# First down projection with tokens as rows and seven block products for 8 of 22 pairs, weight sums in place, result turned back

## The chip, the cores and the metric

The kernel runs on one core of a Trainium2 chip. The metric is the device time of one execution in microseconds (us). TensorE (PE) does the matmuls, VectorE (DVE) and ScalarE (ACT) the elementwise work, GpSimd (POOL) and SyncE (SP) issue most of the transfers. PE reads its operands from SBUF and writes its sums to PSUM.

## The reference

The reference is a decoder trunk of two layers on 256 tokens of width D = 2048: gated linear attention, then block attention over a shared K/V, each followed by a gated feed-forward block with F = 5632 hidden channels. What the change touches is the down projection of the feed-forward block, and what stands behind the first of them:

```
def conv_ffn(x, norm_w, w_up, conv_w, conv_b, w_down):
    ...
    return (jax.nn.silu(a) * u) @ w_down          # (256, 5632) @ (5632, 2048)
...
h = h + conv_ffn(h, ...)                          # layer 0
k_blk, v_blk, k_mean = shared_kv(h, ...)
h = h + moba_mixer(h, ...)                        # layer 1: q = rms_norm(h) @ w_q first
h = h + conv_ffn(h, ...)                          # layer 1
```

All matrices are fp32. The kernel writes each fp32 factor as a high and a low fp32r part and takes three products (high times high, high times low, low times high) for each product of the reference.

## The kernel before, in words

**Weights.** `WeightStream` brings all weights through SBUF in one fixed order. A chunk is a 128x2048 raw tile (`wraw`, 3 buffers, one 1 MB transfer on SP's queue, L75). Each chunk gives two "halves" of 128x1024. A half is split into `whi` (a copy on ACT, L114) and `wlo` (a subtraction on DVE, L115); both come from a pool of 3 buffers. One call of `step()` hands one half to PE, and `prefetch` splits up to 2 halves ahead of PE (3 ahead in the last stage, where every fourth half has a buffer in the big pool instead). `step()` also runs jobs that `after(n, job)` has put down for n steps later.

**First down projection.** `project(rows(hid), FT, ...)` holds channels as rows. For each of 8 pairs of output blocks, `gemm` (L266 to L278) runs over 44 tiles of 128 hidden channels. Per tile and block there is one matmul of 512 columns (L275: 256 tokens high beside 256 tokens low, against `whi`) and one of 256 columns (L276: tokens high against `wlo`). That makes 704 of each. The weights are the stationary operand. After each pair, `residual` adds both PSUM parts to `h` (L309, L310), and `Norm.feed` makes the operand of the next stage, `xw` (ACT L208, DVE L209), and the sum of squares (ACT L218, DVE L219). `h` (8 tiles, in 4 slots) stays in SBUF for the whole kernel.

**The stage behind it.** The q projection is 4 calls of `gemm_tok`, 8 steps each. Step p of each call uses `xw` of pair p only: 12 matmuls of 512 columns (L290 to L292). Two steps in, `n.close` (L538) sums the squares for the norm; one step in, `bias_rows` (L596 to L615) starts. It loads `oh`, has PE make `biasrow` (L603), copies it on ACT (L605), sets part of it on DVE (L606), writes it to DRAM from POOL's queue (L608) and then gathers four tiles of 512 KB from there, also on POOL's queue (L612).

**Second down projection.** `last` (L748 to L811) already holds tokens as rows: the hidden tokens are the stationary operand and 512 columns of weights stream past. Output columns are cut in two blocks b of 1024, and the hidden tiles in 22 pairs k. A plain pair takes 8 block products of 3 matmuls each. In the 8 pairs of `SEVEN_PAIRS` the 2x2 blocks of tokens and weights take 7 products instead (a Strassen-Winograd scheme), so 21 matmuls in place of 24 (L769). This needs sums of token blocks (`combine`, made in the up projection for 4 pairs and at the start of the down projection for the other 4) and sums of weight blocks (`_sum`, L91, L93 and L94, into tiles of their own). A seven pair has four halves: `b11` (512 wide, 3 matmuls), and three of 1024 (6 matmuls each). PSUM holds six sums in the three `acc` tiles and two in the two `bank` tiles.

The order of instructions on each engine is made by a scheduler from the order in which the program is written, dependences and free buffers. Each engine runs its list in order.

Of the kernel before, what the change touches and what calls it, by code (L numbers as in the profile page):

```python
# [35 lines left out]
SEVEN_PAIRS = (1, 3, 6, 8, 11, 13, 16, 18)  # L36
SEVENS = [k in SEVEN_PAIRS for k in range(FT // 2)]
EARLY = 4


class WeightStream:
# [4 lines left out]
    def __init__(self, nc, raw, parts):  # L46
        self.nc, self.raw, self.parts = nc, raw, parts
        self.chunks, self.halves = [], []
        self.tiles, self.split = {}, {}
        self.n_dma = self.n_split = self.n_sum = 0  # L50
        self.cuts, self.lead = {}, {}
        self.sums, self.slot = {}, None
# [8 lines left out]
    def add_quads(self, w, g, kinds):  # L61

        for i, seven in enumerate(kinds):
# [17 lines left out]
    def _sum(self, upto):  # L81

        V = self.nc.vector
        while self.n_sum < min(upto, len(self.halves)):
            c, o, kind = self.halves[self.n_sum]
            if kind in ("t13", "t24"):
                self._dma(c + 1)
                src = self.tiles[c]
                t = self.slot([128, 1024], F32, kind)
                if kind == "t13":  # L90
                    V.tensor_sub(t, src[:, 512:1536], src[:, 0:1024])  # L91
                else:
                    V.tensor_add(t[:, :512], self.sums[self.n_sum - 1][:, 512:], src[:, :512])  # L93
                    V.tensor_sub(t[:, 512:], src[:, 1536:], t[:, :512])  # L94
                self.sums[self.n_sum] = t
            self.n_sum += 1

    def prefetch(self, i):
        nc = self.nc
        while self.n_split < len(self.halves):  # L100
# [5 lines left out]
            self._sum(n + 2)  # L106
            src = self.sums[n] if kind in ("t13", "t24") else self.tiles[c][:, o:o + 1024]
# [5 lines left out]
            for a, b in ((0, 512), (512, 1024)) if n == 0 else ((0, 512 if kind == "b11" else 1024),):  # L113
                nc.scalar.copy(hi[:, a:b], src[:, a:b])  # L114
                nc.vector.tensor_sub(lo[:, a:b], src[:, a:b], hi[:, a:b].bitcast(F32))  # L115
            self.split[n] = (hi, lo)
            self.sums.pop(n - 1, None)
# [11 lines left out]
def trunk(ctx: ExitStack, tc: tile.TileContext, xT, cst, msk, w1p, w2a, w_k, w_qa, w_v, w_g, w_go,  # L129
# [20 lines left out]
    def bank(name, shape):  # L150
# [4 lines left out]
            (w_up0, FT, 4096), (w_dn0, 8, FT * 256),  # L155
            (w_mq, 4, 8192), (w_kk, 4, 8192), (w_kv, 4, 8192), (w_mo, 8, 4096),
            (w_up1, FT, 4096)]
    for w, groups, cols in plan:
        for g in range(groups):
            ws.add(w, g, cols)  # L160
    for g in range(2):
        ws.add_quads(w_dn1, g, SEVENS)
# [396 lines left out]
    def ffn(layer, nrm, then):  # L559
# [5 lines left out]
        for j in range(FT):  # L565
# [18 lines left out]
            if layer == 1 and j % 2 and j // 2 in SEVEN_PAIRS[:EARLY]:  # L584
                combine(j // 2, whole)
        then(hid)

    n_ffn = Norm(C_FN, "xw")
# [143 lines left out]
    hscr = dram.tile([2, 128, D], F32, name="hscr")  # L732

    def turn_h(c, t):

        tp = bank("hT", (128, 512))
        for i in range(4):
            T.transpose(tp[:, 128 * i:128 * i + 128], h[2 * c + i // 2][:, i % 2, 128 * t:128 * t + 128], ident)
        x = temp("hT", (128, 512))
        A.copy(x, tp)  # L740
        nc.gpsimd.dma_start(hscr[t, :, 512 * c:512 * c + 512], x)

# [3 lines left out]

    def last(hid):
        for i, k in enumerate(SEVEN_PAIRS[EARLY:]):  # L748
            after(2 + 3 * i, lambda k=k: combine_parts(k, hid))
        for b in range(2):  # L750
            r = []
            for c in range(2):
                for t in range(2):
                    x = temp("res", (128, 512))
                    nc.gpsimd.dma_start(x, hscr[t, :, 1024 * b + 512 * c:1024 * b + 512 * c + 512])
                    r.append(x)
            two = [acc_ps.tile([128, 2, 512], F32, name="acc") for _ in range(3)]
            p = {n: two[i // 2][:, i % 2, :] for i, n in enumerate((1, 6, 5, 7, 2, 3))}
            p[4], p[8] = bank("p4", (128, 512)), bank("p8", (128, 512))
            left = {1: 0, 2: 0, 3: 0, 4: 0, 5: 0, 6: 0, 7: 0, 8: 0}  # L760
            for seven in SEVENS:
                for n in ((1, 5, 7, 6, 4, 3, 2) if seven else (2, 3, 4, 8, 2, 3, 4, 8)):
                    left[n] += 3
            begun = set()

            def prod(n, x, hi, lo):
                for xp, wp in ((x[0], hi), (x[0], lo), (x[1], hi)):
                    left[n] -= 1
                    T.matmul(p[n], xp, wp, start=n not in begun, stop=left[n] == 0)  # L769
                    begun.add(n)  # L770

            def part(k, i, t):
                x = hid[k][:, i, 128 * t:]
                return x[:, :128], x[:, S:S + 128]

            for k, seven in enumerate(SEVENS):
                if seven:
# [128 lines left out]
```

## Time and profile before

| what | us |
|---|---|
| time, median of 3 runs | 2247.14 (2246.71 to 2247.66) |
| the profiled execution, its own time | 2248.82 |
| span of its profile | 2246.7 |
| PE busy | 2226.4 (99%) |
| DVE busy | 1580.2 (70%) |
| ACT busy | 1232.8 (55%) |

The span is the time from the first to the last profiled instruction, the execution's own time is 2.1 us more. The profile page gives busy times by engine, the chain of work that ended last, and groups of instructions by source line. `us, mean ns | idle before` in a group are total busy time, the mean duration of one, and how long its engine stood still just before.

### The profile page before, as it was taken

The numbers are of one execution on the slowest core, as the hardware profiler recorded it, in microseconds if no ns is written. First come the engines' busy times: TensorE is split into PE (matmuls) and PEld (weight loads), VectorE is DVE, ScalarE is ACT, GpSimd is POOL, SyncE is SP. The second block draws the span as 40 slices with busy tenths as digits, with TensorE's granted clock in tenths as the row PEclk, the third lists the DMA queues.
The fourth block names the chain that finished last, engine by engine and source line by source line (L and its number), as shares of the span: only waits on it lengthen the run. The fifth ranks groups of instructions, "written<-read, shape, count | busy, mean of one in ns | idle before, by whom it ended". The sixth has DMA issues, their size and how long they took to land.

```text
span 2246.7 us, 30752 instructions
## 1 busy us (share of the span) xinstructions
PE 2226.4 (99%) x12146; PEld 1920.2 (85%) x12146; DVE 1580.2 (70%) x2151; ACT 1232.8 (55%) x1717; POOL 35.9 (2%) x43
## 2 busy tenths in 40 slices
PE   7999999999999999999999999999999999999999
PEld 6889888888888888888888888888888888887887
DVE  6566776777777777555557666567777777788876
ACT  6555654655555555444456565456556555555543
POOL 0000000000000000000011000000000000000000
PEclk9999999999999999999999999999999999999999
DMA  6554455555555555555565444456555555555654
GB/s 238 187 188 150 158 184 186 187 193 193 192 189 188 187 189 191 191 194 192 173 237 185 176 169 162 165 193 203 197 188 189 192 193 192 189 188 204 227 190 166
DMA packets 62739, 424.33 MB, mean 189 GB/s; under 512 B 7249, under 2 KB 7777, under 8 KB 13186
## 3 DMA queue, kind: packets, MB, share of 16 engines
q1 hardware_dynamic: 60210, 415.43, 52.3%
q0 software_dynamic: 1952, 6.37, 0.8%
q8 instruction: 95, 1.56, 0.3%
q10 hardware_dynamic: 432, 0.57, 0.1%
q14 instruction: 50, 0.41, 0.1%
HBM read 418.12 MB, written 4.22 MB: 188 GB/s over the span
## 4 chain that ended last, share of the span: by engine, by line
PE 97%; DVE 2%; DMA 1%; issue 0%; ACT 0%; DVEq 0%
PE acc L275 47%; PE acc L276 24%; PE acc L769 5%; PE acc L291 5%; PE acc L292 5%; PE acc L290 5%; PE p L769 3%; DVE wlo L115 1%; DMA wraw<-w_v 0%; PE sT L473 0%; PE tr L636 0%; DMA wraw<-w_dn 0%; PE s L654 0%; ACT whi L114 0%; PE pT L674 0%
## 5 line engine op out<-in xcount | busy, mean ns | idle before, releaser
L115 DVE TENSOR_TENSOR wlo<-wraw,whi 128x1024 fp32r<-128x1024 f32 (+1 forms) x785 | 948.2, 1212 | 550.8 <-ACT whi L114 544.1
L114 ACT CAST whi<-wraw 128x1024 fp32r<-128x1024 f32 (+1 forms) x785 | 814.9, 1042 | 865.6 <-PE acc L275 586.1
L275 PE MATMUL acc<-xw,whi 128*128 128x512 f32 x3328 | 1158.8, 393 | 0.0
L276 PE MATMUL acc<-xw,wlo 128*128 128x256 f32 x3328 | 928.5, 279 | 0.0
L275 PEld LDWEIGHTS acc<-xw,whi 128*128 128x128 f32 x3328 | 623.5, 187 | 141.7
L276 PEld LDWEIGHTS acc<-xw,wlo 128*128 128x128 f32 x3328 | 627.2, 188 | 0.2
L275 PE MATMUL acc<-hid,whi 128*128 128x512 f32 x704 | 244.1, 394 | 0.0
L276 PE MATMUL acc<-hid,wlo 128*128 128x256 f32 x704 | 195.0, 277 | 0.0
L275 PEld LDWEIGHTS acc<-hid,whi 128*128 128x128 f32 x704 | 132.0, 188 | 30.6
L276 PEld LDWEIGHTS acc<-hid,wlo 128*128 128x128 f32 x704 | 132.2, 188 | 0.0
L290 PE MATMUL acc<-whi,xw 128*128 128x512 f32 x256 | 100.7, 393 | 12.1 <-ACT xw L208 12.1
L291 PE MATMUL acc<-wlo,xw 128*128 128x512 f32 x256 | 101.0, 395 | 0.3 <-DVE wlo L115 0.3
L292 PE MATMUL acc<-whi,xw 128*128 128x512 f32 x256 | 100.7, 393 | 0.0
L291 PE MATMUL acc<-wlo,xkv 128*128 128x512 f32 x256 | 100.6, 393 | 0.0
L290 PE MATMUL acc<-whi,xkv 128*128 128x512 f32 x256 | 100.5, 393 | 0.0
L292 PE MATMUL acc<-whi,xkv 128*128 128x512 f32 x256 | 100.4, 392 | 0.0
L769 PE MATMUL acc<-whi,hid 128*128 128x512 f32 x288 | 100.3, 390 | 0.0
L572 ACT ACTIVATE au<-up,cs 128x256 f32<-128x256 f32 x176 | 95.9, 592 | 6.0 <-DVE up L568 6.0
L769 PE MATMUL p<-whi,hid 128*128 128x512 f32 x256 | 91.0, 392 | 0.1
L275 PE MATMUL acc<-go,whi 128*128 128x512 f32 x256 | 90.5, 399 | 0.0
L275 PE MATMUL acc<-ox,whi 128*128 128x512 f32 x256 | 89.1, 394 | 0.0
L574 DVE SCALAR_TENSOR_TENSOR au<-up,cs,au 128x255 f32<-128x255 f32 x176 | 76.9, 478 | 0.0
(238 smaller groups left out, 2231.3 us busy)
## 6 DMA issues: line engine op xcount, KB each, us to landing
wraw<-w_up SPq DMA_DIRECT2D x176, 1024.0 KB, 4.7
wraw<-w_dn SPq DMA_DIRECT2D x84, 1024.0 KB, 4.8
wraw<-w_g SPq DMA_DIRECT2D x16, 1024.0 KB, 4.8
wraw<-w_go SPq DMA_DIRECT2D x16, 1024.0 KB, 4.7
wraw<-w_mq SPq DMA_DIRECT2D x16, 1024.0 KB, 4.8
wraw<-w_kk SPq DMA_DIRECT2D x16, 1024.0 KB, 4.8
wraw<-w_kv SPq DMA_DIRECT2D x16, 1024.0 KB, 4.8
wraw<-w_mo SPq DMA_DIRECT2D x16, 1024.0 KB, 4.8
```

The source lines that it names most:

```text
L114: nc.scalar.copy(hi[:, a:b], src[:, a:b])
L115: nc.vector.tensor_sub(lo[:, a:b], src[:, a:b], hi[:, a:b].bitcast(F32))
L275: T.matmul(ps[:, b, :], hi[:, c:c + 128], x, start=kt == 0, stop=False)
L276: T.matmul(ps[:, b, :S], lo[:, c:c + 128], x[:, :S], start=False, stop=kt == kts - 1)
L290: T.matmul(ps[:, t, :], xh, wh, start=kt == 0, stop=False)
L291: T.matmul(ps[:, t, :], xh, wl, start=False, stop=False)
L292: T.matmul(ps[:, t, :], xl, wh, start=False, stop=kt == KT - 1)
L572: A.activation(au[:, i, :], t[:, i, :], AF.Identity, bias=col(cb + n), scale=col(cw + 2 * 2 * FT + n))
L574: V.scalar_tensor_tensor(au[:, i, 1:], t[:, i, :S - 1], col(cw + 2 * FT + n), au[:, i, 1:], op0=OP.mult, op1=OP.add)
L769: T.matmul(p[n], xp, wp, start=n not in begun, stop=left[n] == 0)
```

## The change

- The first down projection is written like the second one: tokens as rows, two blocks of 1024 output columns, 22 pairs, 8 of them with seven products in each block. Both use the new function `down`. The order of the pairs is written out in `ORDERS`; `+` marks a pair with seven products. In the second down projection the second block has 10 seven pairs, the first 8 as before.
- The weight sums are made in place in the raw tile (`_sums`, four operations of 512 columns on DVE). The halves of a seven pair are taken in another order: `b11`, `wide` (plain b22 and b21), `t13` (b12 and b22 after their sums), `t24` (b11 and b21 after theirs).
- `h` is written to DRAM during the first up projection (`park`, 8 transfers of 256 KB on POOL's queue) and its SBUF slots become free.
- The result of the first down projection has tokens as rows, while the next stage wants channels as rows. `back(q)` turns pair q with four PE transposes, loads the parked `h[q]` on POOL's queue, adds, and feeds the norm. For q = 0 to 3 (block 0) this runs inside block 1, for q = 4 to 7 one and two steps into the q projection. `nrm.close` runs 5 steps in.
- `EARLY`, the pairs whose token sums are made in the up projection, is (1, 3, 5, 7), now in both layers.
- In the second down projection the load of the residual stands behind the last seven pair of a block, no longer at the block's start.

```diff
+EARLY = (1, 3, 5, 7)
+ORDERS = [[_order("0 1+ 2 3+ 4 16 5+ 6 7+ 17 8 9+ 10 11+ 18 12 13+ 14 15+ 19 20 21"),
+           _order("0 2 4 6 8 10 1+ 12 3+ 14 5+ 16 7+ 17 9+ 18 11+ 19 13+ 20 15+ 21")],
+          [_order("0 1+ 2 3+ 4 16 5+ 6 7+ 17 8 9+ 10 11+ 18 12 13+ 14 15+ 19 20 21"),
+           _order("0 1+ 2 3+ 4 5+ 6 7+ 8 9+ 10 11+ 12 13+ 14 15+ 16 17+ 18 19+ 20 21")]]
...
-            self.halves += ([(c, 0, "b11"), (c, 0, "t13"), (c, 0, "t24"), (c, 1024, "wide")] if seven else
+            self.halves += ([(c, 0, "b11"), (c, 1024, "wide"), (c, 512, "t13"), (c, 0, "t24")] if seven else
...
+    def _sums(self, src):
+        V = self.nc.vector
+        b11, b12, b22, b21 = (src[:, 512 * i:512 * i + 512] for i in range(4))
+        V.tensor_sub(b22, b22, b12)
+        V.tensor_sub(b12, b12, b11)
+        V.tensor_add(b11, b22, b11)
+        V.tensor_sub(b21, b21, b11)
...
+    def down(layer, hid, ready, jobs):
+        done = set(EARLY)
+        for b, order in enumerate(ORDERS[layer]):
+            new = [k for k, seven in order if seven and k not in done]
+            done |= set(new)
+            todo = dict(jobs.get(b, {}))
+            for i, k in enumerate(new):
+                todo.setdefault(2 + 2 * i, []).append(late(k))
+            low = acc_ps.tile([128, 2, 512], F32, name="acc")
+            p = {2: low[:, 0], 3: low[:, 1], 4: bank("p4", (128, 512)), 8: bank("p8", (128, 512))}
...
+            for i, (k, seven) in enumerate(order):
+                for job in todo.get(i, ()):
+                    job()
+                if seven:
+                    prod(1, part(k, 0, 0), step(), 0)
+                    w = step()
+                    prod(3, comb(k, 3), w, 0)
+                    prod(2, part(k, 1, 0), w, 1)
...
+                else:
+                    for a in range(2):
+                        w = step()
+                        for n, t, f in ((2, 0, a), (3, 0, 1 - a), (4, 1, a), (8, 1, 1 - a)):
+                            prod(n, part(k, a, t), w, f)
+                if i == last:
+                    sums = ready(b, p)
+            ws.prefetch(cur[0])
+            sums(b, p)
...
+    def park(p):
+        nc.gpsimd.dma_start(hspill[p], h[p].rearrange("a b c -> a (b c)"))
+
+    def first_down(hid, nrm):
+        blocks = {}
+        def ready(b, p):
+            blocks[b] = r = u_sums(p, None)
+            def end(b, p):
+                for x, n in zip(r, (2, 3, 4, 8)):
+                    V.tensor_add(x, x, p[n])
+            return end
+
+        def back(q, where):
+            r = blocks[q // 4]
+            tp = where()
+            c, i0 = q % 4 // 2, q % 2 * 2
+            for i in range(2):
+                for t in range(2):
+                    T.transpose(tp[:, i, 128 * t:128 * t + 128],
+                                r[2 * t + c][:, 128 * (i0 + i):128 * (i0 + i) + 128], ident)
+            if q % 2 == 0:
+                hs[q // 2] = slot([128, 2, 2, S], F32, "h")
+            h[q] = hs[q // 2][:, q % 2]
+            nc.gpsimd.dma_start(h[q], hspill[q].rearrange("a (b c) -> a b c", b=2))
+            V.tensor_add(h[q], h[q], tp)
+            nrm.feed(q)
...
+        down(0, hid, ready, {1: {3 + q: [lambda q=q: back(q, in_acc)] for q in range(4)}})
+        for q in range(4, NP):
+            after(1 + (q - 4) // 2, lambda q=q: back(q, lambda: bank("hf", (128, 2, S))))
+        after(5, nrm.close)
...
     project(rows(go), KT, [n_ffn])
+    for p in range(NP):
+        after(6 + 2 * p, lambda p=p: park(p))
     n_q = Norm(C_MN, "xw", True)
-    ffn(0, n_ffn, lambda hid: project(rows(hid), FT, [n_q]))
+    ffn(0, n_ffn, lambda hid: first_down(hid, n_q))
```

More of the change, by code (lines that the diff above doesn't have):

```diff
@@ L105, in prefetch @@
             self._dma(c + 1)
-            self._sum(n + 2)
-            src = self.sums[n] if kind in ("t13", "t24") else self.tiles[c][:, o:o + 1024]
+            src = self.tiles[c]
+            if kind == "t13":
+                self._sums(src)
+            if kind == "t24":
+                src = src.rearrange("p (a b) -> p a b", a=4)[:, 0::3]
+            elif kind == "b11":
+                src = src[:, :512]
+            else:
+                src = src[:, o:o + 1024]
             if kind != "plain" and n % 4 == 3:
@@ L812, in trunk @@
-    ffn(1, n_ffn, last)
+    ffn(1, n_ffn, last_down)
 def _chunks(w):
```

213 lines of the change are left out of this document (108 added, 105 removed).

## The prediction

> **What bounds the kernel now.** I read the page first: engines, then the chain of work that ended last.
>
> ```profile
> span 2246.7 us, 30752 instructions
> PE 2226.4 (99%) x12146; PEld 1920.2 (85%) x12146; DVE 1580.2 (70%) x2151; ACT 1232.8 (55%) x1717; POOL 35.9 (2%) x43
> PE 97%; DVE 2%; DMA 1%; issue 0%; ACT 0%; DVEq 0%
> ```
>
> PE is busy for 99% of the span and holds 97% of the chain. So a matmul that goes is worth its full time, and a new wait of PE costs its full time. The profiled execution took 2248.82 us, 2.1 more than its span; the sums below stand against it. The median of the three runs, 2247.14, is 1.7 lower, and I give the result on that basis.
>
> Next the table of windows, for the four stages that the change touches: the first down projection, the head of the q projection, and start and middle of the second down projection (the number behind x counts instructions).
>
> ```profile
> core 0: us, PE busy (x) PEld busy (x) DVE busy (x) ACT busy (x) POOL busy (x), PEclk, DMA share, GB/s
> 885.88:1130.00 244.12, 244.12 (x1411) 213.50 (x1410) 129.00 (x131) 103.97 (x114) 0.51 (x1) 1.00 0.54 190
> 1130.00:1150.00 20.00, 20.00 (x91) 15.83 (x90) 11.06 (x15) 12.13 (x16) 3.52 (x5) 1.00 0.55 187
> 2005.60:2032.00 26.40, 23.63 (x94) 17.72 (x93) 26.09 (x44) 14.89 (x20) 0.54 (x1) 0.94 0.38 130
> 2032.00:2168.00 136.00, 136.00 (x601) 112.33 (x600) 111.88 (x121) 69.69 (x74) 2.15 (x4) 1.00 0.59 218
> ```
>
> The first down projection and the head of the q projection have no PE gap. DVE stands at 53% in the first, 82% in the middle of the second, and 99% in the start of the second, where PE falls short. So what the change brings into layer 0 is a stage with little DVE to spare. The waits of PE say that the start is the only place where the existing token-major form stalls:
>
> ```profile
> PE acc L769 <- DVE wlo L115: 2.0, 3, 1.1
> PE acc L769 <- ACT whi L114: 1.2, 1, 1.2
> ```
>
> **The change part by part: matmuls.** By tile `hid`:
>
> ```profile
> L275 PE MATMUL acc<-hid,whi x704: 392/394/395, 885.9 to 1129.6; 128*128 128x512 f32 x176
> L276 PE MATMUL acc<-hid,wlo x704: 274/277/280, 886.2 to 1129.9; 128*128 128x256 f32 x176
> ```
>
> The durations overlap, so I go by pace. Now: 704 pairs in 244.12 us. In the middle window of the second down projection 601 matmuls of 512 columns take 136.00 us, 0.2263 each. Without sevens the new form would have 2 x 22 x 24 = 1056 of them, 239.0 us, 5.1 less. Sixteen seven pairs save 3 each, 48 x 0.2263 = 10.9. Together **-16.0**. In the second down projection two more sevens save 6 x 0.2263 = **-1.4**.
>
> Turning back costs 32 transposes; the nearest row is eight in 0.87 us on the chain of waits, in order of time:
>
> ```profile
> 1138.34 0.74 PE biasrow L603 x2
> 1164.78 0.87 PE tr L636 x8
> ```
>
> 32 x 0.109 = **+3.5**. All removed, added and moved matmuls: **-13.9**.
>
> **Start of the down projection.** In 2005.60 to 2032.00 PE did 94 matmuls, worth 94 x 0.2263 = 21.3 us, in 26.4: 5.1 lost. Three gaps stand in the timeline of PE, and behind them a stretch with a lower granted clock:
>
> ```profile
> 2021.17 0.50 PE L769 MATMUL acc<-wlo,hid 128*128 128x512 f32 x1 [0.48 <-DVE wlo L115]
> ...
> 2024.72 0.51 PE L769 MATMUL acc<-whi,comb 128*128 128x512 f32 x1 [1.21 <-ACT whi L114]
> ...
> 2026.31 0.50 PE L769 MATMUL acc<-wlo,comb 128*128 128x512 f32 x1 [1.08 <-DVE wlo L115]
> ```
> ```profile
> 2027.60:2030.60 3.00, 3.00 (x8) 1.89 (x7) 3.00 (x4) 3.00 (x5) 0.00 (x0) 0.53 0.00 0
> ```
>
> The gaps add to 2.8 us, the clock of 0.53 takes the rest. DVE is the cause: the token sums of four late pairs are made there, each with rows like these:
>
> ```profile
> L556 DVE TENSOR_TENSOR whole<-hid x4: 683/691/693, 2013.9 to 2027.4; 128x512 f32<-128x512 f32 x4
> L544 DVE TENSOR_TENSOR comb<-whole x4: 281/288/293, 2017.1 to 2032.1; 128x128 f32<-128x128 f32 x4
> ```
>
> One late pair is 0.69 + four of 0.28 to 0.29 + a last subtraction of 512 columns, 0.69 (L314): 2.5 us, four pairs 10. The changed program asks for them at pairs 2, 4, 6, 8, but in its built order, in both layers alike, the scheduler puts all four right at the start again. Adding DVE's durations along that list and PE's at 0.2263, the `wlo` of the third pair is ready 2.4 us after PE wants it; the same addition on the kernel before gives 2.0 where 5.1 was measured. So layer 0, which has no such loss now, gets what layer 1 has: I take **+5.5** (bounds: 3, the gaps without the clock, to 8) and **+0.4** for layer 1.
>
> The Trainium skill, "TensorE: Matmul & The Clock Gate", Part 1: The HAM clock gate, says that the clock halves after an idle window of about 3.4 us. By it, gaps that are this short would cost no clock and the start would lose only its gaps, some 2 us less. The rows above speak against it: 0.53 was granted after gaps of at most 1.21 us.
>
> **Alternating pairs.** Behind the start a seven pair and a plain one follow each other. The rows for DVE and ACT:
>
> ```profile
> L115 DVE TENSOR_TENSOR wlo<-wraw,whi 128x1024 fp32r<-128x1024 f32 x767 | 936.3, 1224 | 548.3 <-ACT whi L114 541.6 <-PE acc L276 3.3 <-PE p L769 0.8
> L114 ACT CAST whi<-wraw 128x1024 fp32r<-128x1024 f32 x767 | 803.9, 1052 | 845.5 <-PE acc L275 585.6 <-PE acc L292 111.9 <-ACT au L572 56.6
> L115 DVE TENSOR_TENSOR wlo<-wraw,whi 128x512 fp32r<-128x512 f32 x18 | 12.3, 685 | 2.5 <-ACT whi L114 2.5
> L93 DVE TENSOR_TENSOR t<-t,wraw 128x512 f32<-128x512 f32 x16 | 10.9, 684 | 0.0
> ```
>
> A seven pair takes DVE 0.685 + 3 x 1.224 + 4 x 0.684 = 7.1 us, a plain one 2.45: 9.5. PE takes 45 x 0.2263 = 10.2. Four sums of 512 columns replace one of 1024 and two of 512 (0.2 more by these rows). In place, the first two sums must wait until `wide` has been read, and the copies of `t13` and `t24` wait for them: the chain sum, sum, copy (1.05), subtraction (1.22) is 3.6 us long, the six matmuls per 512-column half and the plain steps in front give 5 or more. It fits, with 1.3 to 1.4 us to spare per two pairs. In layer 1's second block two late pairs (17, 19) come in at 2.5 us each. I take **+1.5** for both layers; bounds 0, and 34 seven pairs x 0.2 = 7. The sums at block ends run on DVE and ACT under the next plain pairs (24 matmuls, 5.4 us, stand ahead of the reused p4, p8).
>
> Transfers of POOL's queue, by the table of DMA issues (the last number is the median time to landing):
>
> ```profile
> bias<-bscr POOLq DMA_DIRECT2D x4, 512.0 KB, 8.3
> hscr<-hT POOLq DMA_DIRECT2D x8, 256.0 KB, 5.2
> res<-hscr POOLq DMA_DIRECT2D x8, 256.0 KB, 3.8
> ```
>
> `park`'s eight transfers, like `hscr` in size and kind, are issued under up projection matmuls that don't read them, and layer 1's later residual load (`res`) has plain steps in front of its first reader: nothing for either, or, uncovered, the 3.8 us of one load.
>
> **The q projection** is where I see the largest new cost. Time 0 is its first matmul in the built order. A step is 12 x 0.2263 = 2.72. Steps 0 to 4 with 8 transposes end at 14.5, `biasrow` (0.74 above) at 15.2, step 5 with the transposes for pairs 6 and 7 at 18.8. Steps 6 and 7 need pairs 6, 7 turned back, and for these the parked `h` must return from DRAM. Their loads stand on POOL's queue behind the bias rows:
>
> ```profile
> 1141.09 0.50 POOL L608 DMA_DIRECT2D bscr<-brow  x1 [39.24 <-DVE sum_parts L314]
> 1146.24 3.02 POOL L612 DMA_DIRECT2D bias<-bscr  x4 [4.66 <-DMA bscr<-brow]
> ```
> ```profile
> DMA to landing us min/median/max: 4.4/8.3/9.4
> ```
>
> `bscr` was issued 2.0 after `biasrow`'s end at 1139.08, the gathers 5.15 later, when it had landed, and their issue took 3.0. So 15.2 + 2.0 = 17.2, + 5.15 = 22.4, + 3.0 = 25.4: only then can POOL issue the two loads of `h`. By themselves they land 3.8 later, at 29.2 (`res`: same size, same queue). Behind 2 MB of gathers, whose last landed 9.4 after issue, they land about 35.5 and 37.
>
> While PE waits for pairs 6 and 7, the order gives it steps 0 to 2 of the second q matrix first. But pairs 6 and 7 hold two of the three buffers of `whi` and `wlo`, so these three steps share one: each must wait for its copy (1.05) and subtraction (1.22) after the step before has ended. That is 2.27 three times, less 0.44 under transposes: 6.4 us of stall in any case, and PE gets there at 18.8 + 8.15 + 6.4 = 33.3. Then with the late landing: add for pair 6 (0.69) and, in DVE's order, for pair 7 (37 + 0.69), then the low part of `xw` (0.48, next row): 38.2.
>
> ```profile
> L209 DVE SCALAR_TENSOR_TENSOR xw<-h,cs,xw 128x256 fp32r<-128x256 f32 x64 | 27.9, 480 | 0.0
> ```
>
> The two steps, but for two matmuls on the high part that go ahead, end at 43.2, where without stalls 32.4 would do: **+10.8** (bounds 6.4, and 15 if the loads land last of all at DRAM speed shared with the weights). Nothing covers it: all later steps in PE's list stand behind. A gap of some 4 us may also lower the clock; **+0.7**, as at the start but mostly hidden under the waiting.
>
> The Trainium skill, "DMA: Bandwidth & Descriptors", Queues, rings and completion order, says that each DMA engine has one ring per queue row and consumes it in ring order, going round between rows by packets. By it, the loads of `h` come behind all four gathers of their row, as in my late landing; no run here shows it yet.
>
> **Sum.** -13.9 + 5.5 + 0.4 + 1.5 + 10.8 + 0.7 = +5.0. 2248.8 + 5.0 = 2253.8 for a profiled execution, and **2252** on the basis of the median.
>
> **The rivals.**
>
> 1. *The loads of `h` come in time* (not slower). If they land within about 5.5 us of issue, before 31, everything behind them is done by the time PE has finished the one-buffer steps at 33.3, and only 6.4 of the 10.8 remain: 2252 - 4.4 = **2247.7**. For it: `res` landed in 3.8, the first gather in 4.4. Against: the median gather took 8.3 on that queue.
> 2. *The chain of in-place sums is late in every seven pair* (slower). With DVE at 93% by these sums and a scheduler that puts other work between, a delay of 0.3 per seven pair over 34 is +10: **2262**. It decides once DVE's work between two pairs passes 10.2 us, 0.7 more than the 9.5 above. Against: the window 2032 to 2168, with sums just as many, shows no PE gap at 82% DVE.
> 3. *The start costs layer 0 little, and the loads come in time* (faster). In layer 0 the stream may be further ahead when the stage starts; with 1 in place of 5.5 and rival 1: **2242** to 2243 or a little less. Against: the same DVE list in both layers.
> 4. *The change doesn't do what it says*: `down` does take fewer matmuls in the built order (1008 in layer 0), so this is left only as unknown faults of the schedule: anywhere, 2 in 100.
>
> **How the numbers follow.** Forecast 0.43 (own range 2249 to 2257, from a landing at 33 to one at 39 and the start's bounds), rival 1 0.25 (2244 to 2250), rival 2 0.18 (2257 to 2266), rival 3 0.12 (2238 to 2243), rival 4 0.02. The measurement can tell 0.2% from no change, 4.5 us: faster lies below 2242.6, slower above 2251.6. Of the forecast a little over six tenths is slower. Slower: 0.27 + 0.18 + 0.02 = 0.47. Faster: most of rival 3, 0.09, and 0.03 of rival 1 and 4: 0.12. Same: 0.41. The range from 2241 to 2264 leaves out the lower third of rival 3 and the top of rival 2 and of the forecast, some 0.12.
>
> **What would show it.** The profile after should have about 1008 matmuls by `hid` and combinations in layer 0 at 0.226 each in a middle window without PE gaps (a steady gap there before `wlo` or `whi`: rival 2); three gaps of 0.5 to 1.3 us about 15 us into the first down projection and a clock below 1 behind them (none: rival 3); in the q projection, three gaps of about 2.3 us before `whi` of one buffer, then one wait of 4 to 5 us on `xw` of pair 6, released by a transfer of `h` on POOL's queue that landed 10 us after issue (3.8 after: rival 1). I would be wrong if the first down projection itself were not some 10 us shorter, or if a stall showed where I have none, at the block ends or in the up projection that now has `park` and the token sums.

## The result and the profile after

| | before | after |
|---|---|---|
| time, median of 6 runs, us | 2247.03 (2246.54 to 2247.66) | 2255.58 (2254.01 to 2258.20) |
| span of the profiled execution, us | 2246.7 | 2253.5 |

The ratio is 1.0039 (95% interval 1.0026 to 1.0052): the changed kernel is 8.5 us slower, where the prediction had 5 us. The page of the changed kernel, the lines that answer to those of before:

```profile
span 2253.5 us, 30247 instructions
PE 2219.5 (98%) x11772; PEld 1900.3 (84%) x11772; DVE 1682.1 (75%) x2339; ACT 1262.2 (56%) x1765; POOL 43.5 (2%) x59
PE 92%; DVE 4%; DMA 2%; ACT 1%; issue 1%; SPq 0%; DVEq 0%; ACTq 0%
```

PE has less to do (374 instructions fewer, transposes counted in), but its share of the chain fell from 97 to 92%: DVE, transfers and ACT now hold PE up. Three windows cut the kernel at the same places before and after: first down projection, everything from the q projection to the end of the second up projection, second down projection. The columns are those of the first table of windows: stretch and its length, busy us of PE, PEld, DVE, ACT and POOL with the number of instructions, granted clock of PE, DMA share, GB/s. Before:

```profile
885.88:1129.99 244.11, 244.11 (x1411) 213.49 (x1409) 129.00 (x131) 103.97 (x114) 0.51 (x1) 1.00 0.54 190
1129.99:2005.94 875.95, 875.95 (x4796) 758.25 (x4795) 624.23 (x923) 506.97 (x765) 27.14 (x24) 1.00 0.54 189
2005.94:2242.05 236.11, 232.73 (x1010) 189.18 (x1008) 190.97 (x219) 117.81 (x128) 2.69 (x5) 0.99 0.53 193
```

And after:

```profile
883.11:1123.74 240.63, 234.60 (x1026) 189.68 (x1025) 200.76 (x244) 123.87 (x143) 3.71 (x7) 1.00 0.55 199
1123.74:2011.61 887.87, 882.63 (x4812) 761.95 (x4811) 631.26 (x937) 509.94 (x774) 25.58 (x23) 1.00 0.55 186
2011.61:2248.56 236.95, 231.01 (x1004) 186.67 (x1002) 208.54 (x260) 119.57 (x134) 4.29 (x8) 1.00 0.54 195
```

So the three stages changed by -3.5, +11.9 and +0.8, together +9.3. (The first one starts 2.8 us earlier after. The first up projection, the only changed part ahead of it, is as long as before, 488.4 us against 488.5 from its first matmul, and in the runs below, whose front part is the same but for a buffer or two, the stage starts between 883 and 886: that is variation, and with it the spans differ by 6.8.) The waits of PE name what is new:

```profile
PE acc L628 <- ACT whi L123: 5.5, 11, 1.3
PE acc L628 <- ACT whi L127: 4.6, 10, 0.9
PE acc L303 <- ACT whi L127: 3.0, 3, 1.1
PE acc L304 <- DVE wlo L128: 2.6, 4, 0.8
```

L628 are the matmuls of both down projections, L303 and L304 those of the q projection. In the timeline of PE the q projection's gaps are these:

```profile
1143.68 0.50 PE L303 MATMUL acc<-whi,xw 128*128 128x512 f32 x1 [0.70 <-ACT whi L127]
1144.94 0.50 PE L304 MATMUL acc<-wlo,xw 128*128 128x512 f32 x1 [0.76 <-DVE wlo L128]
1148.91 0.50 PE L303 MATMUL acc<-whi,xw 128*128 128x512 f32 x1 [1.13 <-ACT whi L127]
1150.17 0.59 PE L304 MATMUL acc<-wlo,xw 128*128 128x512 f32 x1 [0.76 <-DVE wlo L128]
1155.68 0.50 PE L303 MATMUL acc<-whi,xw 128*128 128x512 f32 x1 [1.13 <-ACT whi L127]
1156.94 0.53 PE L304 MATMUL acc<-wlo,xw 128*128 128x512 f32 x1 [0.76 <-DVE wlo L128]
```

Three times whi, then wlo, late by a copy and a subtraction: steps 0 to 2 of the second q matrix in one buffer, as the prediction has it. And behind the second and the third pair of gaps PE ran at half clock (columns as in the windows above, the third from the end is the clock):

```profile
1150.50:1153.70 3.20, 3.20 (x9) 2.46 (x8) 0.00 (x0) 0.00 (x0) 0.11 (x1) 0.50 1.02 333
1157.30:1160.70 3.40, 3.40 (x10) 2.62 (x9) 1.17 (x2) 0.45 (x2) 0.00 (x0) 0.50 0.39 152
```

There is no wait of PE on `xw` of pair 6 or for a transfer of `h`. POOL's queue is as predicted, in its timeline, and behind it DVE's addition in its own:

```profile
1146.50 3.03 POOL L789 DMA_DIRECT2D bias<-bscr  x4 [4.75 <-issue]
1149.52 1.09 POOL L746 DMA_DIRECT2D h<-hspill  x2
```
```profile
1159.53 1.33 DVE L747 TENSOR_TENSOR h<-h,hf 128x512 f32<-128x512 f32 x2 [2.64 <-DMA h<-hspill]
```

DVE waited for the load of `h`, which landed at 1159.5, 10 us after its issue and 35.8 after the stage began at 1123.7 (35.5 in the prediction). `xw` of pair 6 was then made by about 1161, just when PE, slowed by the clock, came for it. The late landing was there and cost nothing that could be seen. Whether it stood ready as the next bound was the question for the experiments.

In the first down projection PE lost, by 240.63 - (1008 x 0.2263 + 16 x 0.109) = 10.8 us: seven gaps of 0.2 to 0.9 from 892 to 908, one of 0.9 at 933, five of 0.2 to 0.6 from 1051 to 1075. The two longest of the first seven:

```profile
894.87 0.50 PE L628 MATMUL acc<-wlo,comb 128*128 128x512 f32 x1 [0.70 <-DVE wlo L124]
904.59 0.50 PE L628 MATMUL acc<-whi,comb 128*128 128x512 f32 x1 [0.91 <-ACT whi L127]
```

The idle times add to 6.0; each gap costs some 0.16 more than it shows, because the end of the matmul in front is modelled 0.39 after its start and the pace is 0.2263. The remaining 2.7 are slightly stretched intervals between matmuls. Away from the gaps the pace is the predicted one:

```profile
945.00:1045.00 100.00, 100.00 (x449) 82.53 (x448) 74.97 (x87) 50.34 (x60) 2.14 (x4) 1.00 0.53 190
```

(433 matmuls x 0.2263 + 16 transposes x 0.109 = 99.7.)

### The profile page after: what moved, and what is told of

The parts are those of the page before. It is cut to its first block, busy times and chain, and to the rows that moved or that the text cites. A ratio compares the mean times of both kernels' runs of the same rounds, so it can differ in the third digit from the quotient of the medians.

```text
span 2253.5 us, 30247 instructions
## 1 busy us (share of the span) xinstructions
PE 2219.5 (98%) x11772; PEld 1900.3 (84%) x11772; DVE 1682.1 (75%) x2339; ACT 1262.2 (56%) x1765; POOL 43.5 (2%) x59
## 4 chain that ended last, share of the span: by engine, by line
PE 92%; DVE 4%; DMA 2%; ACT 1%; issue 1%; SPq 0%; DVEq 0%; ACTq 0%
PE acc L288 39%; PE acc L289 20%; PE acc L628 9%; PE p L628 6%; PE acc L304 5%; PE acc L305 5%; PE acc L303 5%; DVE wlo L128 2%; DMA wraw<-w_dn 1%; ACT whi L127 1%; PE sT L486 0%; ACT whi L123 0%; PE tr L813 0%; DVE wlo L124 0%; DMA wraw<-w_v 0%
## 5 line engine op out<-in xcount | busy, mean ns | idle before, releaser
L128 DVE TENSOR_TENSOR wlo<-wraw,whi 128x1024 fp32r<-128x1024 f32 (+1 forms) x819 | 977.5, 1200 | 478.2 <-ACT whi L127 473.1
L127 ACT CAST whi<-wraw 128x1024 fp32r<-128x1024 f32 (+1 forms) x819 | 839.3, 1033 | 862.0 <-PE acc L288 448.6
L628 PE MATMUL acc<-whi,hid 128*128 128x512 f32 x568 | 203.6, 391 | 1.5 <-ACT whi L127 1.5
L628 PE MATMUL p<-whi,hid 128*128 128x512 f32 x500 | 176.7, 390 | 0.0
L628 PEld LDWEIGHTS acc<-whi,hid 128*128 128x128 f32 x568 | 106.6, 188 | 26.0 <-ACT whi L127 4.0
L303 PE MATMUL acc<-whi,xw 128*128 128x512 f32 x256 | 102.8, 401 | 14.7 <-ACT xw L221 11.7
L628 PE MATMUL acc<-wlo,hid 128*128 128x512 f32 x284 | 110.9, 390 | 0.6 <-DVE wlo L128 0.6
L628 PEld LDWEIGHTS p<-whi,hid 128*128 128x128 f32 x500 | 93.9, 188 | 18.7
L628 PE MATMUL acc<-whi,comb 128*128 128x512 f32 x272 | 98.7, 396 | 8.5 <-ACT whi L123 5.5
L304 PE MATMUL acc<-wlo,xw 128*128 128x512 f32 x256 | 102.5, 401 | 2.6 <-DVE wlo L128 2.6
L304 PE MATMUL acc<-wlo,xkv 128*128 128x512 f32 x256 | 100.6, 393 | 0.0
L303 PE MATMUL acc<-whi,xkv 128*128 128x512 f32 x256 | 100.5, 393 | 0.0
L628 PE MATMUL p<-wlo,hid 128*128 128x512 f32 x250 | 97.3, 389 | 0.0
```

What stands on the lines that cost most here:

```text
L303: T.matmul(ps[:, t, :], xh, wh, start=kt == 0, stop=False)
L304: T.matmul(ps[:, t, :], xh, wl, start=False, stop=False)
```

## The experiments

My theory names three losses: (a) the q projection loses 10 us, because the loads of `h` stand behind the gathers, so that its steps are reordered and share a buffer; (b) the late token sums crowd DVE at the start of both down projections, some 5 us each; (c) the alternating pairs lose some 3 us in each, perhaps because a raw tile that holds its sums in place is released late. Rivals are named with each run. Each ratio is taken against runs of the kernel before that were made together with that run (their median lies between 2246.71 and 2248.78), so ratios are what can be compared between runs.

### The bias rows later

```diff
-    after(1, bias_rows)
+    after(12, bias_rows)
```

> The bias rows start 12 steps into the q projection and not 1, so that the loads of h for pairs 6 and 7 stand ahead of the gathers on POOL's queue; the built order then keeps steps 6 and 7 of the first q matrix in their place, and no step shares a buffer. My theory (the steps that share one buffer, 6.2 us of gaps, and the two stretches at half clock behind them, 3.4 us, are the loss of the q projection, and the place of the loads is why they share): 9.6 us less, about 2246. Rival (the stage loses its time to the turning back itself, to transposes, additions and the norm's operands late in the stage, whatever the order): no change, 2255 to 2256. A second rival (the late bias rows stall the softmax behind them): a loss of a few us in the next stage.

Measured: 2247.86, ratio 0.9993 (0.9984 to 1.0003), against 1.0039. From the q projection to the second down projection:

```profile
1126.80:2004.55 877.75, 877.75 (x4811) 759.82 (x4810) 630.64 (x937) 510.28 (x774) 24.98 (x22) 1.00 0.55 187
```

No gap and 877.75 us: 875.95 of before plus 16 transposes (1.74). In POOL's timeline the loads are now issued right after the slots come free:

```profile
1086.54 1.07 POOL L746 DMA_DIRECT2D h<-hspill  x2 [4.15 <-PE p L628]
```

All of loss (a) is gone, and PE has no gap in the softmax behind it either. But the edit takes away two things at once, the late landing and the reordering. The next run parts them.

### Buffers of their own for steps 6 and 7

```diff
-            if kind != "plain" and n % 4 == 3:
+            if kind != "plain" and n % 4 == 3 or n in self.own:
...
+    q0 = next(i for i, (c, _, _) in enumerate(ws.halves) if ws.chunks[c][0] is w_mq)
+    ws.own = (q0 + 6, q0 + 7)
```

> The bias rows stay where they are, but the whi and wlo of steps 6 and 7 of the first q matrix get tiles of the big pool, so that the second matrix has all three buffers. The loads of h still stand behind the gathers and should land about 10 us after issue, as in the changed kernel. My theory (sharing one buffer is the loss, the late landing alone is hidden): 9.6 us less, about 2246, with no gap above 0.3 us in that stage. Rival (the landing at 35 to 36 us after the stage's start is a bound of its own, and a wait for xw of pair 6 takes the place of the gaps): 4 to 9 us of the gain come back as one wait, 2250 to 2255.

Measured: 2254.45, ratio 1.0025 (1.0015 to 1.0034). The shared buffer's gaps are gone, and one long wait stands in their place:

```profile
1165.52 0.79 PE L306 MATMUL acc<-whi,xw 128*128 128x512 f32 x1 [4.92 <-ACT xw L224]
```
```profile
1165.30:1172.00 6.70, 6.12 (x14) 4.33 (x15) 6.70 (x12) 5.51 (x10) 0.00 (x0) 0.50 0.49 157
1124.98:2011.40 886.42, 881.13 (x4811) 761.59 (x4810) 630.52 (x937) 509.97 (x774) 24.54 (x23) 1.00 0.55 186
```

PE runs ahead through six steps of the second matrix, then stands 4.9 us for pair 6 and runs the next 6.7 us at half clock, which costs some 3.4. The stage is 886.4 against 887.9. My theory, that the landing alone is hidden, falls; the rival holds: shared buffer and late landing are two bounds that lie side by side, and taking one away uncovers the other. The landing itself came later here (the two loads were issued at 1150.8, 25.8 after the stage began as in the changed kernel, landed 13.5 later, and PE could go on at 40.5).

### Plain pairs first

```diff
-ORDERS = [[_order("0 1+ 2 3+ 4 16 5+ 6 7+ 17 8 9+ 10 11+ 18 12 13+ 14 15+ 19 20 21"),
+ORDERS = [[_order("0 2 4 6 8 10 1+ 12 3+ 14 5+ 16 7+ 17 9+ 18 11+ 19 13+ 20 15+ 21"),
```

(and the same for block 1 of layer 1)

> In both layers the first block begins with six plain pairs and then alternates, as the second block of layer 0 does already; the same sevens, the same work. My theory (the late token sums meet the first seven pairs on DVE, and cost 5.2 us in layer 0 and 5.6 us in layer 1 up to the last gap that they touch): 9 to 11 us less, 2245 to 2247. Rival (alternating pairs lose the time wherever they stand, by weights that land late or by a DVE that is too full): the gaps only move behind the plain pairs, 2252 to 2256.

Measured: 2254.03, ratio 1.0024 (1.0014 to 1.0034), 3 us less and not 10. The windows of the two down projections go different ways:

```profile
884.89:1120.47 235.58, 232.87 (x1026) 190.01 (x1025) 200.87 (x244) 124.16 (x143) 3.72 (x7) 1.00 0.56 203
2008.00:2245.68 237.68, 231.25 (x1004) 186.67 (x1002) 209.47 (x260) 120.13 (x134) 4.32 (x8) 1.00 0.54 195
```

In layer 0 the gaps at the start are gone and 5.05 us with them, as theory (b) said. In layer 1 they are gone too, but the block now ends in alternating pairs and the next one starts with more, and six new gaps of 0.2 to 1.4 us stand at that boundary (2127 to 2139). The longest waits for a sum at the block's end, and DVE makes late token sums (those of pairs 17 and 19) at the same place:

```profile
2132.69 0.50 PE L628 MATMUL p<-whi,hid 128*128 128x512 f32 x1 [1.44 <-DVE res L709]
2130.16 0.68 DVE L569 TENSOR_TENSOR whole<-hid 128x512 f32<-128x512 f32 x1
```

So the gaps moved, as the rival says; but they moved to a place where DVE has block-end sums and token sums together, and that alternating pairs lose the time wherever they stand is not shown. A further row bears on the question of the run before. In this kernel one stretch of half clock fell away in the q projection, and at once PE waits for pair 6 behind the shared buffer:

```profile
1157.38 0.50 PE L303 MATMUL acc<-whi,xw 128*128 128x512 f32 x1 [0.98 <-ACT xw L221]
```

That is 36.9 us after the stage began; the prediction had 38.2 for the low part of `xw`, which comes right behind. The same wait stands in three of the runs below, too: 2.32 us with few sevens, 1.85 and 1.22 in the two with sums in tiles of their own, each 36 to 37 us after the stage began. So the late landing does bound PE in these runs, which spent less time at half clock in front of it.

### Few sevens in layer 0

```diff
-ORDERS = [[_order("0 1+ 2 3+ 4 16 5+ 6 7+ 17 8 9+ 10 11+ 18 12 13+ 14 15+ 19 20 21"),
-           _order("0 2 4 6 8 10 1+ 12 3+ 14 5+ 16 7+ 17 9+ 18 11+ 19 13+ 20 15+ 21")],
+ORDERS = [[_order("0 1+ 2 3 4 16 5 6 7 17 8 9 10 11 18 12 13 14 15 19 20 21"),
+           _order("0 2 4 6 8 10 1+ 12 3 14 5 16 7 17 9 18 11 19 13 20 15 21")],
```

> Layer 0 keeps one pair with seven products in each block and takes all others plain (1050 matmuls and not 1008); layer 1 is as in the changed kernel. The token sums of pairs 3, 5 and 7 are still made in the up projection and not used. 42 matmuls more are 9.5 us. My theory (all 8.2 us of PE's loss in the first down projection come with its seven pairs): 9.5 - 8.2 = 1 us more, 2256 to 2258, so that the sevens bring nothing there. Rival (part of the loss comes with the token-major form itself, by the mid-block boundary and the turning back): up to 2265.

Measured: 2256.79, ratio 1.0032 (1.0019 to 1.0046). The first down projection:

```profile
885.91:1126.67 240.76, 240.55 (x1068) 198.38 (x1067) 133.80 (x137) 102.48 (x111) 3.73 (x7) 1.00 0.57 201
```

240.76 with 1050 matmuls against 240.63 with 1008: the 42 matmuls that the sevens save (9.5 us) are lost again in full. 1050 x 0.2263 + 1.74 is 239.4, so the token-major form by itself loses 1.4 at most, and all but that of the 10.8 comes with the sevens, their sums of tokens and of weights together.

### Sums in tiles of their own, twice; a fourth raw buffer

For loss (c). The first of these kernels goes back to the kernel before's `_sum` and its order of halves:

```diff
-            self.halves += ([(c, 0, "b11"), (c, 1024, "wide"), (c, 512, "t13"), (c, 0, "t24")] if seven else
+            self.halves += ([(c, 0, "b11"), (c, 0, "t13"), (c, 0, "t24"), (c, 1024, "wide")] if seven else
...
-        V.tensor_sub(b22, b22, b12)
-        V.tensor_sub(b12, b12, b11)
-        V.tensor_add(b11, b22, b11)
-        V.tensor_sub(b21, b21, b11)
+                    V.tensor_sub(t, src[:, 512:1536], src[:, 0:1024])
...
+                    V.tensor_add(t[:, :512], self.sums[self.n_sum - 1][:, 512:], src[:, :512])
+                    V.tensor_sub(t[:, 512:], src[:, 1536:], t[:, :512])
```

> The weight sums go to tiles of their own again, with the order of halves of the kernel before (b11, t13, t24, wide); pairs, orders, turning back and everything else as in the changed kernel. Theory (in place, a raw tile stays occupied until its t24 half has been split, so the next weight load is issued late and lands after PE wants it: in the alternating pairs ACT waits for the landing of a weight tile for 38 us in all in each layer's down projection, 11.5 in the kernel before): the five gaps of block 2 of layer 0 and the last five gaps of layer 1 go, 2.9 + 3.7 us, ratio to the kernel before 1.001 in place of 1.004; ACT's waiting for weights falls to a third. Rival (DVE is too full in alternating pairs, the landing is a coincidence): the gaps stay, ratio 1.004, for DVE's work is the same but for 0.2 us per pair.

Measured: 2265.23, ratio 1.0075 (1.0058 to 1.0091): slower by 8 us than the changed kernel, which neither side expected. Both down projections are longer:

```profile
885.27:1130.49 245.22, 238.29 (x1026) 191.63 (x1025) 196.12 (x228) 126.00 (x143) 3.71 (x7) 0.99 0.55 195
2017.31:2260.09 242.78, 233.83 (x1004) 187.59 (x1002) 202.83 (x241) 121.18 (x134) 4.28 (x8) 0.99 0.54 191
```

Each holds a gap of 2.72 us and a stretch at half clock (6.8 us long in layer 0, 3.4 in layer 1). The second leaves the sums in place and gives raw tiles a fourth buffer:

```diff
-    big = ctx.enter_context(tc.tile_pool(name="big", bufs=34))
-    raw = ctx.enter_context(tc.tile_pool(name="raw", bufs=3))
+    big = ctx.enter_context(tc.tile_pool(name="big", bufs=32))
+    raw = ctx.enter_context(tc.tile_pool(name="raw", bufs=4))
```

> A fourth buffer for raw weight tiles (the big pool gives 2 of its 34 slots for it), the sums stay in place. Theory (a raw tile held too long delays the loads): the next load no longer waits for the tile, the gaps of the alternating pairs go as in the run with tiles of their own, ratio about 1.001. Rival (DVE too full): the gaps stay, ratio 1.004. If the start of the down projections keeps its gaps (4.2 us each), these are the token sums' alone.

Measured: 2250.78, ratio 1.0018 (1.0008 to 1.0027). The third takes the sums to tiles of their own, as the first, but keeps the changed kernel's order of halves:

```diff
-        V.tensor_sub(b22, b22, b12)
-        V.tensor_sub(b12, b12, b11)
-        V.tensor_add(b11, b22, b11)
-        V.tensor_sub(b21, b21, b11)
+        t13, t24 = self.slot([128, 1024], F32, "t13"), self.slot([128, 1024], F32, "t24")
+        V.tensor_sub(t13, src[:, 512:1536], src[:, 0:1024])
+        V.tensor_add(t24[:, :512], t13[:, 512:], src[:, :512])
+        V.tensor_sub(t24[:, 512:], src[:, 1536:], t24[:, :512])
```

> The weight sums go to tiles of their own, as in the run before that did so (ratio 1.0075), but the halves keep the changed kernel's order: b11, wide, t13, t24. So this differs from the changed kernel in the place of the sums alone. If the order of the halves was what made that run slow (its t13 and t24 come right behind b11, their wlo was waited for 1 us at a time), this one is at 1.001 to 1.004, with ACT's waits for weights low again. If the tiles themselves are (larger sums in one piece, two slots of the big pool), it is as slow as that one, 1.006 to 1.008, and the sums in place are a gain of the change.

Measured: 2254.03, ratio 1.0032 (1.0020 to 1.0044). The waits of ACT and DVE in the first down projection tell whether weights come late. The changed kernel, then tiles of their own in the old order (where DVE, which makes the sums, waits for weights as well), and in the new order:

```profile
ACT whi L127 <- DMA wraw<-w_dn: 38.7, 12, 5.4
```
```profile
ACT whi L123 <- DMA wraw<-w_dn: 10.7, 5, 3.4
DVE t L100 <- DMA wraw<-w_dn: 11.5, 7, 2.5
```
```profile
ACT whi L123 <- DMA wraw<-w_dn: 7.1, 5, 3.5
```

With the fourth buffer neither engine has a wait for `w_dn` left. So the sums in place do hold the raw tiles: with the order kept and tiles of their own, ACT waits for weights a fifth as long (DVE another 0.9), in the old order the two engines together somewhat over half as long. But the time hardly follows. With the order kept, the two down projections are as long as in the changed kernel within 1.2 us:

```profile
883.06:1122.55 239.49, 235.05 (x1026) 191.00 (x1025) 196.79 (x228) 125.97 (x143) 3.71 (x7) 0.99 0.58 202
2010.37:2246.77 236.40, 231.45 (x1004) 186.76 (x1002) 203.66 (x242) 121.94 (x134) 4.31 (x8) 1.00 0.55 196
```

Its gaps are fewer (five in layer 0 in place of 13), and most now stand ahead of `wlo`; in layer 0 a stretch of half clock (905 to 909) takes back some 1.7. The fourth buffer gains 1.4 us in layer 0, where a stretch of half clock (898 to 902) takes some 1.7 back, and 2.7 in layer 1:

```profile
885.95:1125.18 239.23, 235.17 (x1026) 190.74 (x1025) 201.51 (x243) 124.75 (x143) 3.72 (x7) 0.99 0.55 200
...
2011.92:2246.19 234.27, 230.50 (x1004) 186.56 (x1002) 209.99 (x260) 120.64 (x134) 4.30 (x8) 1.00 0.54 193
```

Loss (c) has no single cause that these runs show: late weights are worth 1.4 to 2.7 us in a down projection as measured, some 3 with the clock's part in layer 0 added, and where they are on time gaps ahead of `wlo` are left. The old order of halves costs some 10 us against the run that keeps the new one with the same tiles (1.0075 against 1.0032). The two differ in one more thing, though: in the old order `_sum` runs one half ahead of the split and in two parts, so the order alone is the likely cause and not the only one possible.

### Both cures, and more

The bias rows later, and plain pairs first in layer 0 only:

```diff
-ORDERS = [[_order("0 1+ 2 3+ 4 16 5+ 6 7+ 17 8 9+ 10 11+ 18 12 13+ 14 15+ 19 20 21"),
+ORDERS = [[_order("0 2 4 6 8 10 1+ 12 3+ 14 5+ 16 7+ 17 9+ 18 11+ 19 13+ 20 15+ 21"),
...
-    after(1, bias_rows)
+    after(12, bias_rows)
```

> Two cures together: the bias rows 12 steps into the q projection, and plain pairs first in block 1 of layer 0 only (in layer 1 that order gained nothing). If the two losses are apart from each other, the gains add: 10.1 us in the q projection and 5.1 in the first down projection, 2255.6 - 15.2 = 2240 to 2241, ratio 0.997. Rival (the stages hand a delay on, what one gains the next waits for): less than 10 us in all, 2246 or more.

Measured: 2239.75, ratio 0.9966 (0.9954 to 0.9978). The three windows:

```profile
885.40:1120.12 234.72, 232.90 (x1026) 189.98 (x1025) 200.83 (x244) 124.12 (x143) 4.27 (x8) 1.00 0.57 206
1120.12:1997.85 877.73, 877.73 (x4812) 760.02 (x4810) 630.78 (x937) 510.19 (x774) 24.94 (x22) 1.00 0.55 187
1997.85:2235.32 237.47, 231.74 (x1004) 186.74 (x1002) 208.51 (x260) 119.47 (x134) 4.30 (x8) 1.00 0.54 195
```

The gains add, 240.63 - 234.72 and 887.87 - 877.73, as they should when two stages lose for reasons of their own; nothing is handed on. The same with a fourth raw buffer:

```diff
-    big = ctx.enter_context(tc.tile_pool(name="big", bufs=34))
-    raw = ctx.enter_context(tc.tile_pool(name="raw", bufs=3))
+    big = ctx.enter_context(tc.tile_pool(name="big", bufs=32))
+    raw = ctx.enter_context(tc.tile_pool(name="raw", bufs=4))
```

> As the run before, and with the fourth raw buffer. Theory (late weight loads are the third loss, on top of the other two): 5 to 7 us less again, 2234 to 2236, ratio 0.994. Rival (DVE too full): as the run before, 0.997.

Measured: 2243.25, ratio 0.9979 (0.9969 to 0.9988), 3.5 us worse than without. In layer 1 the buffer gains (234.22 against 237.47), in layer 0 it loses more:

```profile
883.20:1124.90 241.70, 234.97 (x1027) 190.78 (x1025) 201.71 (x243) 126.00 (x143) 4.27 (x8) 0.99 0.55 200
```

New gaps of 0.9 us recur there before a `wlo`, 22 us apart, and one of 2.1 with a stretch of half clock behind it. The order on DVE is another one, and the big pool has two slots less; which of these does it was not tried separately. Last, the bias rows later, plain pairs first in layer 0 as above, and the same order for both blocks of layer 1 (the part for layer 1):

```diff
-          [_order("0 1+ 2 3+ 4 16 5+ 6 7+ 17 8 9+ 10 11+ 18 12 13+ 14 15+ 19 20 21"),
-           _order("0 1+ 2 3+ 4 5+ 6 7+ 8 9+ 10 11+ 12 13+ 14 15+ 16 17+ 18 19+ 20 21")]]
+          [_order("0 2 4 6 8 10 1+ 12 3+ 14 5+ 16 7+ 17 9+ 18 11+ 19 13+ 20 15+ 21"),
+           _order("0 2 4 6 8 10 1+ 12 3+ 14 5+ 16 7+ 17 9+ 18 11+ 19 13+ 20 15+ 21")]]
```

> As the run with both cures (0.9966), and layer 1 takes the order of layer 0 in both blocks: six plain pairs first, 8 sevens in each block (6 matmuls more than the changed kernel's layer 1, 1.4 us). If a block of alternating pairs only needs plain pairs ahead of it, layer 1's down projection, 237.2 us there, comes down to the 234.5 of layer 0 less its 1.7 us of transposes: 233, 4 us less, ratio 0.995. Rival (in layer 1 the gaps come with the residual loads and the sums at the end of block 1, which stay): no gain, 0.9966 or a little above.

Measured: 2236.70, ratio 0.9957 (0.9940 to 0.9974), 10 us faster than the kernel before and the best of all. Against the run with both cures the two intervals overlap, but the window of the second down projection is plain, 230.86 against 237.47, more than the 4 us expected:

```profile
1995.99:2226.85 230.86, 230.36 (x1010) 187.84 (x1008) 195.01 (x234) 116.01 (x128) 4.30 (x8) 1.00 0.56 201
```

One gap of 0.4 us is left in it. But the edit does three things to layer 1's second block at once: six plain pairs stand ahead, two pairs (17 and 19) are no longer sevens, and so their late token sums are not made between the blocks. Plain pairs ahead of the first block alone had gained nothing in layer 1 (the run with plain pairs first), so the gain takes the second block's edit; which of its three parts does it is not shown. Layer 0, now with the same orders and the same 1008 matmuls, is longer:

```profile
883.18:1118.27 235.09, 233.03 (x1027) 189.83 (x1025) 200.78 (x244) 124.13 (x143) 4.27 (x8) 1.00 0.57 206
```

Of these 4.2 us the 16 transposes are 1.7; the other 2.5 go with work that only layer 0 has in its second block, such as turning back and adding `h`, but no run takes that apart. ACT's waits in layer 1's stage:

```profile
ACT whi L127 <- DMA wraw<-w_dn: 34.7, 10, 5.0
```

ACT waits for weights nearly as long as in the changed kernel (38.3 there), and PE hardly notices. So late weights are no loss by themselves; that it takes a DVE that is ahead to cover them is my reading, not shown.

## Why the prediction was right, and where not

The direction was right, and the time came 3.6 us above the forecast, inside its own range. The sum is nearer than its terms, and that is partly luck: the q projection came 1.4 us under its terms, the two down projections together 5.6 over. One sign that the prediction gave for being wrong did show: the first down projection was to be some 10 us shorter, and it is 3.5 shorter, 5.2 without its 16 transposes. In its steps:

- **Matmuls, -13.9.** Right: the pace of 0.2263 holds between the gaps, and with few sevens the stage came within 1.4 of the sum by it.
- **Start, +5.5 for layer 0, +0.4 for layer 1.** Right in size for layer 0: plain pairs first took 5.05 away. The form was another: seven short gaps and one at 933, and no lower clock behind them. I had copied the sum of gaps and clock from layer 1 before; DVE's crowding was the part that carried over, and that more gaps made up for the missing clock is luck.
- **Alternating pairs, +1.5 for both layers.** This term was mis-sized, by more than the whole miss. With 0.5 of it for layer 0, that stage was to lose 6.0 against its matmuls and lost 10.8; layer 1's was to come out even and ended at +0.8. So the term is some 7 us in place of 1.5. I had summed DVE's work over two pairs (9.5 of 10.2 us) and taken the slack as enough. The sums in place also keep a raw tile until its last half is split, which I had left out; the load behind it lands late, and that is worth 1.4 to 2.7 us in each layer by the fourth buffer. The rest stays open. I had also read the waits of before as all at the start; one of them, 0.47 us ahead of a `wlo`, stands at 2188.75, inside the second block, and was a hint that sevens stall elsewhere, too. Rival 2 had the place right and put a price of 10 on it, for 34 sevens alike; it came in a few spots.
- **The q projection, +10.8 and +0.7 for the clock.** 10.1 lost (887.87 - 877.75). POOL's queue, the reordering, the one buffer and the landing at 35.5 all came as worked out. The one buffer's gaps are 5.2 us of idle time, 6.2 with 0.16 for each, where I had 6.4. The wait of 4 to 5 us on `xw` of pair 6, which the prediction named as a sign, did not come in this run: two stretches of 3.4 us at half clock, some 3.4 us of PE's time in place of 0.7, stood in its place, and by the end of them `xw` was ready. So the mechanism is right up to the two bounds, and that the clock took nearly as much as the wait would have is luck; in the four runs with less of the clock the wait is there, at 1.0 to 2.3 us, shorter than I had it. Rival 1 needed a landing before 31: it was at 35.8, and at 39 in the second run.
- **`park`, the residual load, the block's middle in layer 0, at nothing.** Right: the first up projection, with `park` and the token sums in it, is as long as before (488.4 and 488.5), and the window from 945 to 1045 with the block boundary in it has no gap.

Two rules of the Trainium skill stood in the prediction. "DMA: Bandwidth & Descriptors", Queues, rings and completion order, has descriptors consumed in ring order on each DMA engine (it says so of the queues of SP and ACT), so that the loads of `h` come behind the gathers. The trace agrees for POOL's queue in the order: the last gather landed at 1158.9, the two loads at 1159.5 and 1160.2, 10 us after issue, where the six loads without gathers in front took 2.9 to 7.0. How much of the ten is the queue and how much the DMA engines, which were fully busy from 1150 to 1157 (a share of 1.02), no run separates. "TensorE: Matmul & The Clock Gate", Part 1, gives an idle window of about 3.4 us as what halves the clock: here it halved behind gaps of 1.13 and 0.76 us, so the rule as stated is not what the runs show.

## What to carry to other kernels

When a stage is forecast to wait, write down every bound that ends near the same time: curing one of two side by side gains little (1.5 of 10 us here), and the cheap cure is the one at their common root, here the place of two loads in a queue. Where an engine has 7% to spare on average, ask which buffer is held longer by the change and what the first pairs find already queued; a run of cheap steps ahead of the dense ones (six plain pairs) was worth 5 us in layer 0. In layer 1 it gained nothing in the first block alone, and 6.6 with the second block changed too, where two sevens and their token sums went as well. And fewer matmuls are worth their time only where the engines that feed them are ahead: 42 fewer gained nothing until the order was changed, then 5 to 6 us.

## What the runs showed of the hardware

- **The clock.** Stretches at half clock were 3.4 us long, or 6.7 to 6.8 (behind gaps of 4.92 and 2.72 us). The same six gaps of 0.7 to 1.13 us, in three pairs, drew two stretches in the changed kernel, one in three other runs (plain pairs first, the fourth buffer, tiles of their own in the new order) and none in two (few sevens, tiles of their own in the old order), up to the wait for pair 6. Seven gaps of 0.2 to 0.9 at the start of a down projection drew none in the changed kernel, and in the run with the fourth buffer three such gaps of 0.33, 0.21 and 0.69 drew one. So the length of the gaps alone doesn't settle it; what does is open.
- **A queue's last transfer.** In the changed kernel four gathers of 512 KB and two loads of 256 KB on one queue landed in order, the loads 10 us after issue. In the run with buffers of their own it took 13.5, with a weight transfer of 1 MB issued at 1154.8 that landed in between, at 1163.5.
- **A gap's price.** A gap of PE costs some 0.16 us more than the idle time shown, by the modelled end (0.39 after its start) of the matmul in front of it, where the pace is 0.2263.
